# A hybrid attention block on one core: 184 TensorE transposes replaced by VectorE block transposes with a transfer between partitions, and the two ends of SBUF exchanged

## The chip, the cores and the metric

The kernel runs on one core of one Trainium2 chip. The metric is the device time of one execution in microseconds (us), lower is better.

## The reference, cut to what matters

One layer of a hybrid block on 256 tokens of 2048 channels, all in float32. Three mixers read the same projection: sparse attention (NSA), a state-space mixer (SSD) and retention. Their results are merged by gates, added to the residual, and a gated feed-forward layer (FFN) with 5632 hidden channels follows.

```
u = rms_norm(x, norm_mix)
proj = u @ w_in                                   # 2048 x 16952
y_nsa, y_ssd, y_ret = nsa(..), ssd(..), retention(..)
g_nsa, g_ssd, g_ret = split(sigmoid(merge_g), 3)
merged = g_nsa*(y_nsa @ p_nsa) + g_ssd*(y_ssd @ p_ssd) + g_ret*(y_ret @ p_ret)
x = x + merged @ w_out
f = rms_norm(x, norm_ffn)
x = x + (silu(f @ w_gate) * (f @ w_up)) @ w_down
return rms_norm(x, norm_final)
```

## The kernel before

**Streams.** Every large product is a call of `stream` (L182 to L227): 256 tokens times a strip of up to 512 columns of one weight matrix. The weights come from HBM in tiles `raw` of 256 rows by 512 columns (0.5 MB, SP's queue, four buffers). ScalarE (ACT) rounds a tile to a short format, `wh` (L134, `act`), VectorE (DVE) subtracts for the rest, `wl` (L209); `wh` and `wl` have four buffers each. Activations stand in the same way as a pair, transposed so that channels lie on partitions: `uh`/`ul` (normed input), `ysh`/`ysl` (SSD), `ynh`/`ynl` (NSA), `yrh`/`yrl` (retention), `mh`/`ml` (merged), `fh`/`fl` (FFN input), `hh`/`hl` (FFN hidden). For each 128 channels and each half of the tokens TensorE (PE) does three matmuls at L221: high by high, high by low, low by high; the activations are the operand that stays in the array, 512 columns of `wh` or `wl` pass through. A tile of weights so feeds 12 matmuls. The names in a profile row are output<-weights,activations.

The order of the streams: the projections for SSD (with the four SSD groups in between), for NSA, then `merge` of SSD (with NSA's attention in between), the projections for retention, `merge` of NSA and of retention, `w_out`, eleven pairs of `w_gate` and `w_up`, and `w_down` in four strips of 44 times 128 channels.

**Side tasks.** Work beside the streams is written as generators in the queues `urgent`, `steady` and `slow`; after each third matmul `pump` takes one step. A step is one small matmul or transpose; `pause(n)` lets n steps pass. A scheduler then orders each engine's instructions by its own clock; each engine runs its list in order.

**Transposes.** A result comes out with tokens on partitions and has to be turned before it is an operand of the next stream. `to_features` (L238, SSD result `y`, retention result `yy`, residual `x2`) and `task_halves` (L894, `merged` and FFN hidden `hb`) do it for 512 channels by eight PE transposes of 128x128 in float32 (L163, tiles `tf` and `hv`) into PSUM; ACT then writes the high part and DVE the low part. There are 4 such turns for SSD, 2 for retention, 4 for `merged`, 4 for `x2` and 11 for `hb`.

**Places in SBUF.** Pools are stacks that grow from the left end (low addresses) or, with `side="right"`, from the right end (the top, 224 KB in a partition). In the built program before, the weights `raw`, `wh`, `wl` lie at 20 to 68 KB, `uh`/`ul` and `fh`/`fl` at 68 to 100, `ynh`/`ynl` at 116 to 132; on the right lie `ysh`/`ysl` at 192 to 224, `yrh`/`yrl` at 208 to 224, `mh`/`ml` at 176 to 208, `hh` at 136 to 180 and `hl` at 180 to 224. In NSA's attention the operands lie at 136 to 181 (keys and queries) and 144 to 160 KB (values and probabilities).

Of the kernel before, what the change touches and what calls it, by code (L numbers as in the profile page):

```python
# [10 lines left out]
F32 = mybir.dt.float32  # L11
# [89 lines left out]
def _build(tc, a):  # L101
# [13 lines left out]
        p = es.enter_context(tc.tile_pool(name=name, bufs=bufs, **kw))  # L115
        return p, es

    cp, _c = pool("const")
    ctx.enter_context(_c)
    rawp, _c = pool("raw", 4)  # L120
    ctx.enter_context(_c)
    hlp, _c = pool("hl", 4)
    ctx.enter_context(_c)
# [9 lines left out]
    def act(out, in_, func, **kw):  # L133
        nc.scalar.activation(out, in_, func, **kw)  # L134
# [53 lines left out]
    def pause(n):  # L188
        for _ in range(n):
            yield  # L190
# [58 lines left out]
                V.scalar_tensor_tensor(dl[:, k, :], pv, sv, dh[:, k, :], OP.mult, OP.subtract)  # L249


    uh = ap_.tile([P, KD, S], F32R, tag="ah", name="uh")
    ul = ap_.tile([P, KD, S], F32R, tag="al", name="ul")
    xt_pool, xt_es = pool("xt")
    xT = xt_pool.tile([P, KD, S], F32, name="xT")
    xsq = xt_pool.tile([P, 2, S], F32, name="xsq")
    xTr = a["xT"].rearrange("(k p) t -> p k t", p=P)
# [37 lines left out]
        stream(uh, ul, KD, w_in, c0, n, evac, **kw)  # L295


    bp, b_es = pool("bigT", side="right")
    ysh = bp.tile([P, KD, S], F32R, tag="bh", name="ysh")
    ysl = bp.tile([P, KD, S], F32R, tag="bl", name="ysl")  # L300
    np1, np1_es = pool("nsa1", side="right")

    def evac_to(get, scale=None):
        box = []
# [69 lines left out]
        square_x(k)  # L374
    row_norm(hps[1][0][:, 256:258])
    xt_es.close()
    sp_, s_es = pool("ssd")
# [151 lines left out]
    def task_z(g, zg):  # L529
        y = ys[g]  # L530
        sq = sp_.tile([P, 4], F32, tag="sq", name="sq")
        for t in range(NT):
            th = sp_.tile([P, 512], F32, tag="th", name="thz", bufs=2)
            act(th, zg[:, t, :], AF.Tanh)
            V.scalar_tensor_tensor(zg[:, t, :], th, 1.0, zg[:, t, :], OP.add, OP.mult)
            V.tensor_tensor(y[:, t, :], y[:, t, :], zg[:, t, :], OP.mult)
            act(zg[:, t, :], y[:, t, :], AF.Square, accum_out=sq[:, t:t + 1])
        rsqrt(sq[:, 2:4], sq[:, 0:2], 1.0 / 512, EPS)
        for t in range(NT):
            V.tensor_scalar(y[:, t, :], y[:, t, :], sq[:, 2 + t:3 + t], None, OP.mult)  # L540
        yield from pause(14)
        yield from to_features(y, 0, R("ssdn"), 4 * g, ysh, ysl, 4 * g)

    for g in range(4):
        steady.append(task_decay(g))
# [22 lines left out]
    kTl = np2.tile([P, 2, 2, S], F32R, name="kTl")
# [329 lines left out]
    def task_halves(src, c0, dh, dl, k0, scale):  # L898
        yield from pause(6)
        for t in range(NT):  # L900
            ps = aux("hv")
            for b in range(4):
                transpose(ps[:, b * P:(b + 1) * P], src[:, t, c0 + b * P:c0 + (b + 1) * P])
                yield
            pv = ps.rearrange("p (b q) -> p b q", b=4)
            o = (slice(None), slice(k0, k0 + 4), slice(t * P, (t + 1) * P))
            act(dh[o], pv, AF.Copy, scale=scale)
            if scale == 1.0:
                V.tensor_tensor(dl[o], pv, dh[o], OP.subtract)
            else:  # L910
                V.scalar_tensor_tensor(dl[o], pv, scale, dh[o], OP.mult, OP.subtract)
# [10 lines left out]

    def open_x2():
        g_es.close()
        ny_es.close()
        m_es.close()
        x2p, box["x2es"] = pool("x2")
# [3 lines left out]
        box["tmp"], box["tmpes"] = pool("ftmp")  # L931

    def task_f(c):
        yield from pause(4)
        yield from to_features(box["x2"], c * 512, R("nffn"), c * 4, fh, fl, c * 4)

    for c in range(4):
        cs = slice(c * 512, (c + 1) * 512)

        def ev_o(t, ps):  # L940
            if c == 0 and t == 0:
                open_x2()
            x2 = box["x2"]
            V.tensor_tensor(x2[:, t, cs], x2[:, t, cs], ps, OP.add)
# [15 lines left out]
    hl = hp_.tile([P, KF, S], F32R, name="hl")  # L960
    for i in range(11):
        hbox = []

        def ev_g(t, ps):
            if not hbox:
                hbox.append(tmp_p.tile([P, NT, 512], F32, tag="hb", name="hb", bufs=2))
            th = tmp_p.tile([P, 512], F32, tag="jk", name="fth", bufs=2)
            act(th, ps, AF.Tanh, scale=r2[:, 1, t:t + 1])
            V.scalar_tensor_tensor(hbox[0][:, t, :], th, 1.0, ps, OP.add, OP.mult)
        stream(fh, fl, KD, a["w_gate"], i * 512, 512, ev_g)  # L970
        hb = hbox[0]

        def ev_u(t, ps):
# [72 lines left out]
```

## Time and profile before

| | |
|---|---|
| time, median of 3 runs | 1860.78 us (1860.46 to 1861.12) |
| the profiled execution | 1862.26 us, of which 1860.5 us are the span of its instructions |
| PE busy | 1848.1 us, 99% of the span |
| DVE, ACT, POOL busy | 1044.0 us (56%), 855.0 us (46%), 59.8 us (3%) |
| HBM read | 342.35 MB, 185 GB/s over the span |

The span runs from the first to the last instruction of one execution. An engine is busy while an instruction of it runs; matmuls overlap, so that the start of one to the start of the next says what one costs, and its length does not.

### The profile page before, as it was taken

Reading aid. Unit: us, or ns where it says so; the run is one execution under the profiler, and the core shown is the slowest. Engines: PE = TensorE matmul, PEld = TensorE weight load, DVE = VectorE, ACT = ScalarE, POOL = GpSimd, SP = SyncE. Lnnn points to the kernel's source line nnn. Section 1 sums busy time; section 2 is a strip of 40 time slices with the busy share of each in tenths; the row PEclk is TensorE's granted clock in tenths of the full one; section 3 lists DMA queues with packets and bytes.
Section 4 is the critical chain, followed back from the end, with each engine's and each line's share of the span. In section 5 each row is a group of like instructions: output and inputs, shape, how many; then the busy total and the mean of one; then the engine's idle time right before and its main releaser. Section 6 shows DMA issues by size and latency. Waiting matters only on the chain.

```text
span 1860.5 us, 22303 instructions
## 1 busy us (share of the span) xinstructions
PE 1848.1 (99%) x8584; PEld 1521.1 (82%) x8584; DVE 1044.0 (56%) x1209; ACT 855.0 (46%) x1092; POOL 59.8 (3%) x75
## 2 busy tenths in 40 slices
PE   9999999999999999999999999999999999999998
PEld 8878888987877888888888888888888888888886
DVE  7688875456555445544555555555555555544443
ACT  7555554454544444544444444444444444443442
POOL 0000001000000001010100100000000000000000
PEclk9999999999999999999999999999999999999999
DMA  9466655754545665666666656666666666655554
GB/s 343 116 210 185 182 160 151 230 170 148 155 149 176 188 179 168 184 194 193 193 186 185 227 181 191 191 186 190 192 183 191 189 186 191 212 186 190 191 188 132
DMA packets 176539, 345.95 MB, mean 186 GB/s; under 512 B 10880, under 2 KB 17152, under 8 KB 175792
## 3 DMA queue, kind: packets, MB, share of 16 engines
q1 hardware_dynamic: 173312, 331.60, 59.0%
q0 software_dynamic: 2688, 12.23, 1.9%
q8 instruction: 67, 1.10, 0.2%
q10 hardware_dynamic: 432, 0.70, 0.1%
q14 instruction: 40, 0.33, 0.1%
HBM read 342.35 MB, written 2.13 MB: 185 GB/s over the span
## 4 chain that ended last, share of the span: by engine, by line
PE 98%; DVE 1%; issue 0%; ACT 0%; POOLq 0%; POOL 0%; DVEq 0%
PE mp L221 90%; PE hp L370 3%; PE yd L518 1%; PE hv L163 1%; PE c L619 1%; PE tf L163 0%; PE pT L163 0%; PE cv L163 0%; PE ny L585 0%; DVE erow L477 0%; PE ny L587 0%; PE ny L589 0%; PE hp L345 0%; PE yo L523 0%; DVE wl L209 0%
## 5 line engine op out<-in xcount | busy, mean ns | idle before, releaser
L209 DVE TENSOR_TENSOR wl<-raw,wh 128x1024 fp32r<-128x1024 f32 (+2 forms) x616 | 748.4, 1216 | 717.5 <-ACT wh L134 717.0
L134 ACT ACTIVATE wh<-raw 128x1024 fp32r<-128x1024 f32 (+2 forms) x616 | 646.6, 1050 | 839.9 <-PE mp L221 776.1
L221 PE MATMUL mp<-wh,uh 128*128 128x512 f32 (+2 forms) x1024 | 408.1, 401 | 0.0
L221 PE MATMUL mp<-wl,uh 128*128 128x512 f32 (+2 forms) x1024 | 396.3, 387 | 2.1 <-DVE wl L209 2.1
L221 PE MATMUL mp<-wh,ul 128*128 128x512 f32 (+2 forms) x1024 | 396.2, 387 | 0.0
L221 PE MATMUL mp<-wh,fh 128*128 128x512 f32 x704 | 281.6, 400 | 0.0
L221 PE MATMUL mp<-wh,fl 128*128 128x512 f32 x704 | 274.5, 390 | 0.0
L221 PE MATMUL mp<-wl,fh 128*128 128x512 f32 x704 | 274.3, 390 | 0.0
L221 PEld LDWEIGHTS mp<-wh,uh 128*128 128x128 f32 x1024 | 193.3, 189 | 40.3 <-issue 1.6
L221 PEld LDWEIGHTS mp<-wh,ul 128*128 128x128 f32 x1024 | 193.1, 189 | 38.2 <-issue 0.7
L221 PEld LDWEIGHTS mp<-wl,uh 128*128 128x128 f32 x1024 | 193.5, 189 | 36.4 <-DVE wl L209 2.5
L221 PEld LDWEIGHTS mp<-wh,fh 128*128 128x128 f32 x704 | 132.2, 188 | 32.0
L221 PEld LDWEIGHTS mp<-wh,fl 128*128 128x128 f32 x704 | 132.2, 188 | 27.9
L221 PEld LDWEIGHTS mp<-wl,fh 128*128 128x128 f32 x704 | 132.5, 188 | 24.2
L221 PE MATMUL mp<-wh,hh 128*128 128x512 f32 x352 | 139.5, 396 | 0.0
L221 PE MATMUL mp<-wh,hl 128*128 128x512 f32 x352 | 138.9, 395 | 0.0
L221 PE MATMUL mp<-wl,hh 128*128 128x512 f32 x352 | 138.9, 395 | 0.0
L221 PEld LDWEIGHTS mp<-wh,hh 128*128 128x128 f32 x352 | 66.3, 188 | 15.8
L221 PEld LDWEIGHTS mp<-wh,hl 128*128 128x128 f32 x352 | 66.3, 188 | 15.6
L221 PEld LDWEIGHTS mp<-wl,hh 128*128 128x128 f32 x352 | 66.3, 188 | 15.1
L221 PE MATMUL mp<-wh,mh 128*128 128x512 f32 x128 | 52.5, 410 | 0.0
L221 PE MATMUL mp<-wh,ysh 128*128 128x512 f32 x128 | 51.1, 399 | 0.0
(300 smaller groups left out, 1655.9 us busy)
## 6 DMA issues: line engine op xcount, KB each, us to landing
raw<-in_w_in_dram SPq DMA_DIRECT2D x240, 512.0 KB, 3.6
raw<-in_w_gate_dram SPq DMA_DIRECT2D x88, 512.0 KB, 3.7
raw<-in_w_up_dram SPq DMA_DIRECT2D x88, 512.0 KB, 3.7
raw<-in_w_down_dram SPq DMA_DIRECT2D x88, 512.0 KB, 4.7
raw<-in_p_ssd_dram SPq DMA_DIRECT2D x32, 512.0 KB, 3.7
raw<-in_w_out_dram SPq DMA_DIRECT2D x32, 512.0 KB, 4.3
raw<-in_p_nsa_dram SPq DMA_DIRECT2D x16, 512.0 KB, 3.8
raw<-in_p_ret_dram SPq DMA_DIRECT2D x16, 512.0 KB, 3.7
```

Source lines behind the costliest of these rows:

```text
L134: nc.scalar.activation(out, in_, func, **kw)
L163: nc.tensor.transpose(out, in_, ident[:n, :n])
L209: V.tensor_tensor(wl[:, ks, :n], raw[:, ks, :n], wh[:, ks, :n], OP.subtract)
L221: mm = nc.tensor.matmul(o, xx[:, k, ts], ww[:, kk, :n], start=(k == 0 and i == 0), stop=(k == K - 1 and i == 2))
L370: nc.tensor.matmul(hps[c][t][:, 0:n], xx[:, k, ts], ww[:, c0:c0 + n], start=(k == 0 and i == 0), stop=(k == KD - 1 and i == 2))
L518: nc.tensor.matmul(ps[:, h * 64:(h + 1) * 64], erow[:, h, t, :], xdt[:, t, h * 64:(h + 1) * 64], start=True, stop=True)
L619: nc.tensor.matmul(ps[:, 0:NC2], wq[:, l, :], blk[b][:, 8 * q + l, :], start=(q == 0 and l == 0), stop=(q == 3 and l == 7))
```

## The change

Two things change.

1. **Sides.** The pools `const`, `raw`, `xt`, `ssd`, `merge`, `mgate`, `nsa2`, `x2` and `ftmp` go to the right end, and `bigT`, `nsa1`, `rety`, `ret`, `mT` and `hT` to the left. NSA's result (`nsay`) is opened before `bigT`, so it lies lowest of these. In the built program `wh`/`wl` now lie at 16 to 48 KB, `uh`/`ul` and `fh`/`fl` at 48 to 80, `ynh`/`ynl` at 80 to 96, `ysh`/`ysl` at 96 to 128, `yrh`/`yrl` at 96 to 112, `mh` at 112 to 128, `ml` at 128 to 144, `hh` at 80 to 124, `hl` at 124 to 168, `raw` at 204 to 220 KB.
2. **Turns.** Of the 25 turns 23 are done by a new `task_exchange`: all of SSD, retention and `hb`, and the first three quarters of `merged` and `x2`. DVE transposes 32x32 blocks of 512 channels into `tq` (two instructions, one for each half of the tokens), 16 transfers on POOL's queue of 32 rows of 1 KB each move the blocks to their partitions (`st_x`), and after `pause(24)` DVE applies the scale where there is one, ACT writes the high part and DVE the low part, now from SBUF and for 1024 elements at once. The last quarters of `merged` and `x2` keep PE's transposes. The factor 0.5 of `merged` moves to the addition after `w_out`, an instruction that is there anyway.

```
-    cp, _c = pool("const")
+    cp, _c = pool("const", side="right")
-    rawp, _c = pool("raw", 4)
+    rawp, _c = pool("raw", 4, side="right")
...
+    def exchange(pl, src, queue, tag="tq", bufs=1):
+        tq = pl.tile([P, 4, 8, 32], F32, tag=tag, name="tq", bufs=bufs)
+        st = pl.tile([P, 4, 8, 32], F32, tag="xs", name="st_x", bufs=1)
+        for t in range(NT):
+            V.transpose(tq.rearrange("p b (f t) q -> p t f b q", t=NT)[:, t], src[:, t, :].rearrange("p (f b q) -> p f b q", f=4, b=4))
+        for x in range(4):
+            for b in range(4):
+                queue.dma_start(st[32 * b:32 * b + 32, x], tq[32 * x:32 * x + 32, b])
+        return st
...
+    def task_exchange(pl, src, dh, dl, k0, scale=None, gap=24, **kw):
+        st = exchange(pl, src, nc.gpsimd, **kw)
+        yield from pause(gap)
+        oh, ol = quarters(dh, k0, 4), quarters(dl, k0, 4)
+        if scale is not None:
+            for f in range(4):
+                v = st.rearrange("p a (f t) q -> p f a (t q)", f=4)[:, f]
+                V.tensor_scalar(v, v, scale[:, f:f + 1], None, OP.mult)
+        act(oh, st, AF.Copy)
+        V.tensor_tensor(ol, st, oh, OP.subtract)
...
-    bp, b_es = pool("bigT", side="right")
+    nyp, ny_es = pool("nsay")
+    bp, b_es = pool("bigT")
...
-        yield from pause(14)
-        yield from to_features(y, 0, R("ssdn"), 4 * g, ysh, ysl, 4 * g)
+        yield from task_exchange(sp_, y, ysh, ysl, 4 * g, R("ssdn")[:, 4 * g:4 * g + 4])
...
-        yield from pause(8)
-        yield from to_features(yy, c * 512, R("retn"), 4 * c, yrh, yrl, 4 * c)
+        yield from task_exchange(rp, yy[:, :, cs], yrh, yrl, 4 * c, R("retn")[:, 4 * c:4 * c + 4])
...
-    mtp, mt_es = pool("mT", side="right")
+    mtp, mt_es = pool("mT")
...
+        if c < 3:
+            yield from pause(2)
+            yield from task_exchange(mtp, merged[:, :, c * 512:(c + 1) * 512], mh, ml, c * 4)
+            return
...
-    hp_, h_es = pool("hT", side="right")
+    hp_, h_es = pool("hT")
...
-        urgent.append(task_halves(hb, 0, hh, hl, 4 * i, 1.0))
+        urgent.append(task_hidden(hb, i))
```

On PE, in the second `w_gate` strip of the FFN, before (operands: `cst` holds the identity, `hb` the hidden channels of the strip ahead; eight rows of `hv` stand in the strip, two are shown):

```order
L221 MATMUL mp_9132<-wh,fh 128x512
L221 MATMUL mp_9132<-wl,fh 128x512
L221 MATMUL mp_9132<-wh,fl 128x512
L163 MATMUL hv<-cst,hb 128x128
L221 MATMUL mp_9131<-wh,fh 128x512
L221 MATMUL mp_9131<-wl,fh 128x512
L221 MATMUL mp_9131<-wh,fl 128x512
L163 MATMUL hv<-cst,hb 128x128
```

In the change no row of `hv` with `hb` is left on PE; of its rows in all, 8133 become 8001 as the listing counts them (runs of the same row counted once).

On DVE, at the same place, before (L974 is the end of a `w_up` strip, L909 writes the low part of the turned strip, L969 is the end of the next `w_gate` strip):

```order
L974 SCALAR_TENSOR_TENSOR hb<-hb,r_8109,mp_8984 128x512
L209 TENSOR_TENSOR wl<-raw,wh 128x1024 x3
L909 TENSOR_TENSOR hl<-hv,hh 128x4x128
L209 TENSOR_TENSOR wl<-raw,wh 128x1024
L909 TENSOR_TENSOR hl<-hv,hh 128x4x128
L209 TENSOR_TENSOR wl<-raw,wh 128x1024 x4
L969 SCALAR_TENSOR_TENSOR hb<-fth,mp_9131 128x512
```

and now (L1010, L1005 and L277 are the lines that answer to L974, L969 and L909):

```order
L1010 SCALAR_TENSOR_TENSOR hb<-hb,r_8181,mp_9080 128x512
L257 STREAM_TRANSPOSE tq<-hb 128x4x4x32
L209 TENSOR_TENSOR wl<-raw,wh 128x1024
L257 STREAM_TRANSPOSE tq<-hb 128x4x4x32
L209 TENSOR_TENSOR wl<-raw,wh 128x1024 x7
L1005 SCALAR_TENSOR_TENSOR hb<-fth,mp_9227 128x512
L209 TENSOR_TENSOR wl<-raw,wh 128x1024
L1005 SCALAR_TENSOR_TENSOR hb<-fth,mp_9228 128x512
L277 TENSOR_TENSOR hl<-st_x,hh 128x4x8x32
```

The two transposes stand right behind the end of `w_up`, and eight weight tiles lie between the second of them and the first use of what the transfers bring. ACT's reader (`hh<-st_x`) stands at the same place. Between transposes and first use lie 7 to 10 weight tiles in all 23 turns; the shortest, 7, is that of the first half of retention:

```order
L257 STREAM_TRANSPOSE tq<-yy 128x4x4x32 x2
L209 TENSOR_TENSOR wl<-raw,wh 128x1024 x7
L902 SCALAR_TENSOR_TENSOR rg<-rth,rg 128x512 x2
L903 TENSOR_TENSOR yy<-yy,rg 128x512
L275 TENSOR_SCALAR st_x<-st_x,prm 128x4x64 x4
```

On POOL the transfers stand between its other work, in the stretch from the merge of retention to the end (before, this list had no L260 rows; `merged` is the addition of a gated product, `x` the residual's load):

```order
L260 DMA st_x<-tq 32x256 x16
L815 TENSOR_TENSOR merged<-merged,gt 128x512 x2
L956 DMA x_8347<-in_x_dram 128x2x512 x4
L260 DMA st_x<-tq 32x256 x48
L167 TENSOR_SCALAR r_8181<-r_8181 128x2
L168 TENSOR_TENSOR r_8181<-r_8181,mhalf 128x2
L260 DMA st_x<-tq 32x256 x160
L1016 DMA nfb<-in_norm_final_dram 128x2048
L260 DMA st_x<-tq 32x256 x16
```

In that list every transfer from the ninth of a turn on waits for the one eight places before it to land, and the first of a turn waits for the readers of the turn before, since `st_x` has one buffer in each pool.

## Rows read from the trace of the kernel before

**Rows 1.** The page: busy time by engine; the chain that ended last, by engine.
```profile
PE 1848.1 (99%) x8584; PEld 1521.1 (82%) x8584; DVE 1044.0 (56%) x1209; ACT 855.0 (46%) x1092; POOL 59.8 (3%) x75
PE 98%; DVE 1%; issue 0%; ACT 0%; POOLq 0%; POOL 0%; DVEq 0%
```

**Rows 2.** Groups by line: PE's matmuls with `wl`, count, busy us, mean ns.
```profile
L221 PE MATMUL mp<-wl,fh 128*128 128x512 f32 x704 | 274.3, 390 | 0.0
L221 PE MATMUL mp<-wl,hh 128*128 128x512 f32 x352 | 138.9, 395 | 0.0
L221 PE MATMUL mp<-wl,ysh 128*128 128x512 f32 x128 | 50.5, 395 | 0.0
L221 PE MATMUL mp<-wl,mh 128*128 128x512 f32 x128 | 50.4, 394 | 0.0
L221 PE MATMUL mp<-wl,yrh 128*128 128x512 f32 x64 | 25.2, 394 | 0.0
L221 PE MATMUL mp<-wl,ynh 128*128 128x512 f32 x64 | 24.9, 389 | 0.0
L587 PE MATMUL ny<-pT,vth 128*128 128x512 f32 x12 | 4.7, 394 | 0.0
```

**Rows 3.** Stretches: busy us and count by engine, granted clock; NSA's merge, then `w_down`.
```profile
782.00:902.00 120.00, 120.00 (x531) 99.36 (x530) 60.04 (x52) 50.60 (x51) 14.11 (x8) 1.00 0.65 193
1640.00:1840.00 200.00, 200.00 (x863) 162.14 (x862) 95.68 (x88) 79.63 (x84) 0.00 (x0) 1.00 0.58 184
```

**Rows 4.** Timeline of PE: start, length; first transposes of some turns.
```profile
299.71 1.03 PE L163 MATMUL tf<-cst,y 128*128 128x128 f32 x8
300.58 0.60 PE L163 MATMUL kc<-cst,kc 128*128 128x128 f32 x4
...
1050.20 0.27 PE L163 MATMUL tf<-cst,x 128*128 128x128 f32 x1
...
1073.38 0.27 PE L163 MATMUL tf<-cst,x 128*128 128x128 f32 x1
...
1164.14 0.27 PE L163 MATMUL hv<-cst,hb 128*128 128x128 f32 x1
...
1208.70 0.27 PE L163 MATMUL hv<-cst,hb 128*128 128x128 f32 x1
```

**Rows 5.** Groups by line: DVE and ACT instructions like those added and removed.
```profile
L909 DVE TENSOR_TENSOR hl<-hv,hh 128x512 fp32r<-128x512 f32 x22 | 15.2, 692 | 0.9
L134 ACT ACTIVATE hh<-hv 128x512 fp32r<-128x512 f32 x22 | 13.2, 600 | 14.6 <-PE hv L163 14.6
L540 DVE TENSOR_SCALAR y<-y,sq 128x512 f32<-128x512 f32 x8 | 3.5, 483 | 1.7 <-POOL sq L168 1.7
```

**Rows 6.** Timelines of ACT and DVE in a `w_gate` strip; brackets: idle before, releaser.
```profile
1148.69 1.06 ACT L134 ACTIVATE wh<-raw 128x1024 fp32r<-128x1024 f32 x1 [1.66 <-PE mp L221]
1149.79 1.23 DVE L209 TENSOR_TENSOR wl<-raw,wh 128x1024 fp32r<-128x1024 f32 x1 [1.50 <-ACT wh L134]
```

**Rows 7.** Timeline of POOL: start, length; issues of transfers, and two arithmetic instructions.
```profile
88.39 0.71 POOL L441 DMA_DIRECT2D adram<-act_t  x1 [30.49 <-DVE act_t L440]
303.39 0.56 POOL L613 DMA_DIRECT2D w<-in_cmp_v_w_dram  x1
330.31 0.88 POOL L617 DMA_DIRECT2D wq<-in_cmp_v_w_dram  x1 [3.75 <-DMA wq<-in_cmp_k_w_dram]
693.56 0.58 POOL L168 TENSOR_TENSOR bn<-bn,mhalf 128x1 f32<-128x1 f32 x1
695.64 1.43 POOL L168 TENSOR_TENSOR bn<-bn,mhalf 128x1 f32<-128x1 f32 x1
```

**Rows 8.** Transfers: KB each, median us from issue to landing.
```profile
wq<-in_cmp_v_w_dram POOLq DMA_DIRECT2D x4, 512.0 KB, 5.3
adram<-act_t POOLq DMA_DIRECT2D x1, 32.0 KB, 2.5
```

More of the change, by code (lines that the diff above doesn't have):

```diff
@@ L249, in to_features, with quarters @@
                 V.scalar_tensor_tensor(dl[:, k, :], pv, sv, dh[:, k, :], OP.mult, OP.subtract)
+    def exchange(pl, src, queue, tag="tq", bufs=1):
[7 more added lines that the diff above has]
+        return st
+    def quarters(d, k, n):
+        return d[:, k:k + n, :].rearrange("p f (t a q) -> p a (f t) q", t=NT, a=4)
+    def task_exchange(pl, src, dh, dl, k0, scale=None, gap=24, **kw):
[8 more added lines that the diff above has]
+        V.tensor_tensor(ol, st, oh, OP.subtract)
     uh = ap_.tile([P, KD, S], F32R, tag="ah", name="uh")
     ul = ap_.tile([P, KD, S], F32R, tag="al", name="ul")
-    xt_pool, xt_es = pool("xt")
+    xt_pool, xt_es = pool("xt", side="right")
     xT = xt_pool.tile([P, KD, S], F32, name="xT")
@@ L295, in proj @@
         stream(uh, ul, KD, w_in, c0, n, evac, **kw)
-    bp, b_es = pool("bigT", side="right")
+    nyp, ny_es = pool("nsay")
+    bp, b_es = pool("bigT")
     ysh = bp.tile([P, KD, S], F32R, tag="bh", name="ysh")
     ysl = bp.tile([P, KD, S], F32R, tag="bl", name="ysl")
-    np1, np1_es = pool("nsa1", side="right")
+    np1, np1_es = pool("nsa1")
     def evac_to(get, scale=None):
@@ L376, in _build @@
     xt_es.close()
-    sp_, s_es = pool("ssd")
+    sp_, s_es = pool("ssd", side="right")
     bt = sp_.tile([P, NT, 512], F32, tag="t4a", name="bt")
@@ L558, in _build @@
     s_es.close()
-    mpool, m_es = pool("merge")
+    mpool, m_es = pool("merge", side="right")
     merged = mpool.tile([P, NT, D], F32, name="merged")
-    nyp, ny_es = pool("nsay")
     ynh = nyp.tile([P, 8, S], F32R, name="ynh")
     ynl = nyp.tile([P, 8, S], F32R, name="ynl")
-    gp, g_es = pool("mgate")
-    np2, np2_es = pool("nsa2")
+    gp, g_es = pool("mgate", side="right")
+    np2, np2_es = pool("nsa2", side="right")
     kTh = np2.tile([P, 2, 2, S], F32R, name="kTh")
@@ L802, in _build @@
     b_es.close()
-    ryp, ry_es = pool("rety", side="right")
+    ryp, ry_es = pool("rety")
     yrh = ryp.tile([P, 8, S], F32R, name="yrh")
     yrl = ryp.tile([P, 8, S], F32R, name="yrl")
-    rp, r_es = pool("ret", side="right")
+    rp, r_es = pool("ret")
     cstr = rp.tile([P, _CSTR.shape[1]], F32, name="cstr")
@@ L893, in _build, with task_merged @@
     r_es.close()
-    mtp, mt_es = pool("mT", side="right")
+    mtp, mt_es = pool("mT")
     mh = mtp.tile([P, KD, S], F32R, name="mh")
     ml = mtp.tile([P, KD, S], F32R, name="ml")
-    def task_halves(src, c0, dh, dl, k0, scale):
+    def task_merged(c):
+        if c < 3:
+            yield from pause(2)
+            yield from task_exchange(mtp, merged[:, :, c * 512:(c + 1) * 512], mh, ml, c * 4)
+            return
         yield from pause(6)
@@ L902, in task_halves @@
             for b in range(4):
-                transpose(ps[:, b * P:(b + 1) * P], src[:, t, c0 + b * P:c0 + (b + 1) * P])
+                transpose(ps[:, b * P:(b + 1) * P], merged[:, t, (4 * c + b) * P:(4 * c + b + 1) * P])
                 yield
             pv = ps.rearrange("p (b q) -> p b q", b=4)
[L906 to L911, printed above, removed]
+            o = (slice(None), slice(4 * c, 4 * c + 4), slice(t * P, (t + 1) * P))
+            act(mh[o], pv, AF.Copy)
+            V.tensor_tensor(ml[o], pv, mh[o], OP.subtract)
     merge(2, yrh, yrl, 8, a["p_ret"],
-          after=lambda c: urgent.append(task_halves(merged, c * 512, mh, ml, c * 4, 0.5)))
+          after=lambda c: urgent.append(task_merged(c)))
     fh = ap_.tile([P, KD, S], F32R, tag="ah", name="fh")
@@ L924, in open_x2 @@
         g_es.close()
-        ny_es.close()
         m_es.close()
-        x2p, box["x2es"] = pool("x2")
+        x2p, box["x2es"] = pool("x2", side="right")
         box["x2"] = x2p.tile([P, NT, D], F32, name="x2")
@@ L930, in open_x2 @@
             nc.gpsimd.dma_start(box["x2"][:, :, c * 512:(c + 1) * 512], xres[:, :, c * 512:(c + 1) * 512])
-        box["tmp"], box["tmpes"] = pool("ftmp")
+        box["tmp"], box["tmpes"] = pool("ftmp", side="right")
     def task_f(c):
-        yield from pause(4)
-        yield from to_features(box["x2"], c * 512, R("nffn"), c * 4, fh, fl, c * 4)
+        if c < 3:
+            yield from pause(2)
+            yield from task_exchange(box["tmp"], box["x2"][:, :, c * 512:(c + 1) * 512], fh, fl, c * 4,
+                                     R("nffn")[:, 4 * c:4 * c + 4], tag="hb", bufs=2)
+        else:
+            yield from pause(4)
+            yield from to_features(box["x2"], c * 512, R("nffn"), c * 4, fh, fl, c * 4)
     for c in range(4):
@@ L943, in ev_o @@
             x2 = box["x2"]
-            V.tensor_tensor(x2[:, t, cs], x2[:, t, cs], ps, OP.add)
+            V.scalar_tensor_tensor(x2[:, t, cs], ps, 0.5, x2[:, t, cs], OP.mult, OP.add)
             jk = box["tmp"].tile([P, 512], F32, tag="jk", name="jk", bufs=2)
@@ L957, in _build, with task_hidden @@
     ry_es.close()
-    hp_, h_es = pool("hT", side="right")
+    ny_es.close()
+    hp_, h_es = pool("hT")
     hh = hp_.tile([P, KF, S], F32R, name="hh")
     hl = hp_.tile([P, KF, S], F32R, name="hl")
+    def task_hidden(hb, i):
+        yield from pause(2)
+        yield from task_exchange(tmp_p, hb, hh, hl, 4 * i, tag="hb", bufs=2)
     for i in range(11):
```

## The prediction

> **What bounds the kernel now.** I read the page first. PE is busy for 99% of the span, and the chain of work that ended last runs 98% through PE [rows 1]. No stage waits for weights, DVE or ACT, so the time is the sum of what PE's instructions cost one after the other. A microsecond comes off only if PE gets fewer instructions or cheaper ones, and added work elsewhere costs only where PE comes to wait for it.
>
> What a matmul costs is read from starts, not lengths. A stretch of the stretches view counts matmuls that reach into it, so its width plus one length (0.39 us) over the count is the pitch: in NSA's merge (120.00 + 0.39) / 531 = 0.2267 us, in `w_down` (200.00 + 0.39) / 863 = 0.2322 us [rows 3]. Both have a granted clock of 1.00, so the 5.5 ns between them are not the clock. The groups by line show the same split in the lengths: 389 to 390 ns with `fh` and `ynh` as activations, 394 to 395 ns with `ysh`, `yrh`, `mh`, `hh` [rows 2]. The split follows the tile: within one merge it changes with the stream. What the slow tiles have in common is their place. All of them lie on the right, at 136 KB or higher; the fast ones lie on the left and end at 132 KB. NSA's own products, with both operands at 144 to 160 KB, have 394 ns too [rows 2]. What differs otherwise (length of the stream, who wrote the tile, the work of DVE and ACT beside it) is the same for some fast and slow tile.
>
> **The change part by part.**
>
> *Removed transposes.* 23 of 25 turns leave PE, eight transposes each, 184. Their cost on the path is again read from starts. In SSD eight stand back to back: from 299.71 to the next instruction at 300.58, 0.87 us [rows 4]. In the FFN a turn begins every 44.56 us (1164.14 to 1208.70 [rows 4]) with 192 matmuls between; 192 x 0.2267 = 43.53, so a turn costs 1.03 us. Among the slow matmuls of `w_out` it is 1050.20 to 1073.38, 23.18 us [rows 4], less 96 x 0.2322 = 22.29, so 0.89 us. I give SSD's 4 turns 0.87 each (3.5), the 4 that stand in slow streams (3 of `x2`, the last of `hb`) 0.89 (3.6), and the other 15 (retention, `merged`, `hb`) 1.03 (15.5). Sum: 22.5 us. Were all at the lowest price it would be 20.0, at the highest 23.7.
>
> *Places.* `ysh`/`ysl` feed 4 x 96 matmuls, `yrh`/`yrl` 4 x 48, `mh`/`ml` 4 x 96, `hh`/`hl` 4 x 264: 2016. Were they all to fall to the fast pitch, 2016 x 5.5 ns = 11.1 us. Somewhere between 132 and 136 KB the price changes; I take 134. In the changed program `ysh`, `ysl`, `yrh`, `yrl`, `mh` and `hh` lie below it. Of `ml` (128 to 144 KB) 10 of 16 channel blocks lie above, of `hl` (124 to 168) 34 of 44: 80 + 272 = 352 matmuls stay slow if the price belongs to the single matmul. 1664 x 5.5 ns = 9.2 us. No row shows fast and slow mixed; if one slow operand spoils its whole group of three, another 2 x 352 x 5.5 ns = 3.9 us stay and the term is 5.3. Ends: 0 and 11.1; I take 9.2.
>
> *DVE and ACT.* The block transpose stands in no row. Per 128x512 I bound it by 0.48 us (one input) and 1.23 us (a weight tile, twice the size), and take 0.69, the price of a 128x512 result of this shape [rows 5, 6]. An FFN turn then costs DVE 2 x 0.69 + 1.23 in place of 2 x 0.69, so 1.2 us more in 44 us, in a stage where it has half its time free (60.04 of 120 busy [rows 3]). ACT writes 1024 elements in 1.06 us in place of 2 x 0.60 [rows 5, 6]. Cost 0, covered by the lead of these engines: ACT starts a weight tile the moment PE frees its buffer, DVE ends it at 1149.79 + 1.23 = 1151.02, and PE has three more tiles of 12 x 0.2267 = 2.72 us to go through, to 1148.69 + 8.16 = 1156.85 [rows 6]. The lead is 5.8 us; a stall of DVE or ACT longer than that reaches PE.
>
> *The transfers.* They are what could make such a stall: ACT and DVE run in order, and `wh` and `wl` of the following tiles are queued behind the instruction that waits for `st_x`. An issue on POOL of the same shape (32 rows of 1 KB) took 0.71 us and landed in 2.5; others took 0.56 and 0.88, the slowest landing is 5.3 [rows 7, 8]. A turn is 16 x 0.71 + 2.5 = 13.9 us after the transposes; bounds 16 x 0.56 + 2.5 = 11.5 and 16 x 0.88 + 5.3 = 19.4. Waiting for the transfer eight places earlier adds nothing as long as eight issues (4.5 us and more) outlast most of a landing. Seven tiles of weights lie between at the least, 19.0 us, in the FFN eight, 21.8 us. So even the upper bound overruns the shortest gap by 0.4 us, inside the lead. Cost 0. POOL's own work is pushed back by one turn (11 us) at most: the additions to `merged` come every 33 us, the residual's load stands ahead of its transfers, and the load for the last norm is needed only in `w_down`. If the lead were gone, a turn late by d would cost d each time.
>
> *The rest.* The factor 0.5 moves into an addition that is there anyway: 0. The scale costs DVE four short instructions where the transposes' eviction had it: in the lead.
>
> Sum: 22.5 + 9.2 = 31.7 us less. Against the profiled execution's own 1862.26 us (span 1860.5 and 1.8 around it) that is 1830.6. The median of the runs shown is 1.5 us below it (1860.78), so I forecast **1829 us** for the median.
>
> **Rivals.**
>
> 1. *The place does nothing*: the 5.5 ns come from something else that goes with these tiles, and only the transposes count. 1860.8 - 22.5 = 1838. For it: no row shows one tile at two places. Against it: nine kinds of operand fall on the right side of one boundary. The Trainium skill, "SBUF — State Buffer", section "Who interferes with whom", speaks for this rival: TensorE has its own read ports and waits for nobody, and it names no cost of an address. By that page the sum would be 22.5 us alone. The trace has two pitches at one clock that the page does not explain, so I believe the rows.
>
> 2. *Mixed streams stay slow* (the group of three): 1860.8 - 22.5 - 5.3 = 1833.
>
> 3. *The transfers come late, and the kernel is slower.* One mechanism: POOL's issues are held up beside DVE. For it: the same small instruction on POOL took 0.58 and 1.43 us [rows 7], so something there can hold POOL for 0.85 us. Were each issue 0.71 + 0.85 = 1.56 us, an FFN turn would take 16 x 1.56 + 2.5 = 27.5 us against 21.8 + 5.8 = 27.6 that are covered: just nothing. From there each 0.1 us more per issue costs 1.6 us a turn and 37 us over 23. At 1.65 us the gain is gone; at 1.8 us (16 x 1.8 + 2.5 - 27.6 = 3.7 us x 23 = 85) the time would be 1860.8 - 31.7 + 85 = 1914. Against it: the issues shown took 0.56 to 0.88 beside the same DVE work. The Trainium skill, the same page, section "SBUF: two separate sides", warns of this trap: transfers issued from POOL need it to write descriptors, and DVE instructions in a two-port mode lock it out. No run shown here lengthens an issue that way.
>
> 4. *Part of the gain is lost to new stalls* in the SSD groups, where DVE is busiest and the scheduler has dealt out all side work anew, or to a late turn now and then: 1840 to 1857.
>
> **How the numbers follow.** A difference of 0.2% (3.7 us) is about what a measurement of this kernel can tell from none. Chances: the forecast (1826 to 1832) 0.55; rival 1 0.2; rival 2 0.12; rival 4 0.07; rival 3 0.06. The range of 8 in 10 must take in the forecast, rival 2 and most of rival 1, with the ends of the transposes' price: at the bottom all tiles fast and the highest price, 1860.8 - 23.7 - 11.1 = 1826; at the top rival 1 with the lowest price, 1860.8 - 20.0 = 1841. I give 1825 to 1841. The first three cases are faster by over 0.2%, and rival 4 nearly so; with a little left for it at the bound, faster 0.93, within 0.2% 0.02, slower 0.05.
>
> **What would show it.** PE with 184 fewer matmuls and still 99% busy; turns that begin 43.5 us apart in the FFN. `mp<-wl,ysh`, `yrh`, `mh` and `hh` at 389 ns instead of 394, `w_down` at a pitch of 0.2267 to 0.229; lengths of 394 there are rival 1, and a pitch of 0.230 or more with `hl` mixed in rival 2. Issues of `st_x` at 0.6 to 0.9 us, and ACT and DVE with no wait for `st_x` above a few us in all; waits of 6 us or more at each turn, followed by PE waiting for `wl`, are rival 3. Wrong would be a PE that waits for `wh` or `wl` in the SSD groups, or transposes of DVE far above 1.2 us.

## Result and the profile after

The change takes 1827.21 us (median of 4 runs, 1825.79 to 1828.67) against 1860.70 us before (median of 4 runs, 1860.46 to 1861.12): ratio 0.982, 95% interval 0.9803 to 0.9837, 33.5 us less. The forecast was 1829 us, with a range of 1825 to 1841. The profiled execution took 1825.79 us with a span of 1823.7, where that of before took 1862.26 with 1860.5: as it happens the one lies 1.4 us under its median and the other 1.6 us over, so between the two traces there are 36.5 us.

The page of the change, busy time by engine and then the chain that ended last, answers to [rows 1]:

```profile
PE 1811.7 (99%) x8400; PEld 1502.6 (82%) x8400; DVE 1069.6 (59%) x1250; ACT 847.2 (46%) x1051; POOL 243.4 (13%) x443
PE 96%; issue 2%; DVE 1%; DMA 0%; POOL 0%; ACT 0%; POOLq 0%; DVEq 0%
```

PE has 184 instructions fewer and 36.4 us less to do. Outside its busy time the span has 12.0 us, before it had 12.4. The "issue 2%" that the chain now names is so no new idle time, only another way in which the chain was put down. So all that was won is work that PE no longer has, and nothing of it was given back as a wait.

The matmuls with `wl` in the groups by line, as in [rows 2]:

```profile
L221 PE MATMUL mp<-wl,fh 128*128 128x512 f32 x704 | 274.0, 389 | 0.0
L221 PE MATMUL mp<-wl,hh 128*128 128x512 f32 x352 | 137.0, 389 | 0.0
L221 PE MATMUL mp<-wl,ysh 128*128 128x512 f32 x128 | 49.9, 390 | 0.0
L221 PE MATMUL mp<-wl,mh 128*128 128x512 f32 x128 | 49.8, 389 | 0.0
...
L221 PE MATMUL mp<-wl,ynh 128*128 128x512 f32 x64 | 24.9, 389 | 0.0
L221 PE MATMUL mp<-wl,yrh 128*128 128x512 f32 x64 | 24.9, 389 | 0.0
```

All are at 389 to 390 ns; the split of [rows 2] is gone. The stretches of NSA's merge and of `w_down`, as in [rows 3], say the same in starts:

```profile
767.00:877.00 110.00, 110.00 (x487) 91.11 (x486) 57.78 (x53) 48.24 (x49) 12.15 (x8) 1.00 0.66 197
1580.00:1780.00 200.00, 200.00 (x884) 165.64 (x883) 98.45 (x91) 82.77 (x87) 7.05 (x15) 1.00 0.64 199
```

(110.00 + 0.39) / 487 = 0.2267 us and (200.00 + 0.39) / 884 = 0.2267 us. `w_down`, which had 0.2322, holds 884 matmuls in the 200 us where it held 863. The low parts stand in the groups with `wh`; `hl` and `ml`, the two tiles that reach highest, are as fast as the others:

```profile
L221 PE MATMUL mp<-wh,hl 128*128 128x512 f32 x352 | 137.0, 389 | 0.0
...
L221 PE MATMUL mp<-wh,ml 128*128 128x512 f32 x128 | 49.9, 389 | 0.0
```

The turns in the FFN, on POOL's timeline (start, length, count, and in brackets the idle time before and what ended it):

```profile
1144.00 5.48 POOL L260 DMA_DIRECT2D st_x<-tq  x11 [44.70 <-ACT wh L134]
1149.80 2.45 POOL L260 DMA_DIRECT2D st_x<-tq  x5 [0.32 <-DMA st_x<-tq]
1187.50 5.45 POOL L260 DMA_DIRECT2D st_x<-tq  x11 [35.26 <-ACT wh L134]
```

A turn begins every 1187.50 - 1144.00 = 43.50 us, where [rows 4] had 44.56: the 192 matmuls between two turns cost 43.53 and nothing else is left on PE. The prices of the new work, which no row of before held, stand in the groups by line: the issues on POOL, and DVE's block transpose of half a strip of `hb` (one half of the tokens).

```profile
L260 POOL DMA_DIRECT2D st_x<-tq x368 | 182.0, 502 | 479.4 <-ACT wh L134 360.9 <-DVE tq L257 39.9 <-DVE fl L277 29.4
...
L257 DVE STREAM_TRANSPOSE tq<-hb 128x512 f32<-128x512 f32 x22 | 15.4, 702 | 0.0
```

The list of issues (KB each, median us to landing) has the transfer itself:

```profile
st_x<-tq POOLq DMA_DIRECT2D x368, 32.0 KB, 4.0
```

The transpose took 0.70 us (0.69 was taken), an issue 0.50 (0.71 was taken from [rows 7]), a landing 4.0 (2.5 was taken from [rows 8]). One turn: 16 x 0.50 + 4.0 = 12.0 us behind the transposes, where 13.9 was worked out. In the list of waits (us in total, times, longest) PE has two in all, and the one for the transfers is POOL's own, for the transfer eight places earlier:

```profile
POOL st_x L260 <- DMA st_x<-tq: 19.7, 40, 1.1
...
PE mp L221 <- DVE wl L209: 1.7, 1, 1.7
...
PE hp L374 <- DVE idle L289: 1.3, 1, 1.3
```

### The profile page after: what moved, and what is told of

Its sections match the earlier page's. It is cut to its first block, busy times and chain, and to the rows that moved or that the text cites. A ratio compares the mean times of both kernels' runs of the same rounds, so it can differ in the third digit from the quotient of the medians.

```text
span 1823.7 us, 22560 instructions
## 1 busy us (share of the span) xinstructions
PE 1811.7 (99%) x8400; PEld 1502.6 (82%) x8400; DVE 1069.6 (59%) x1250; ACT 847.2 (46%) x1051; POOL 243.4 (13%) x443
## 3 DMA queue, kind: packets, MB, share of 16 engines
q0 software_dynamic: 14464, 24.31, 4.0%
## 4 chain that ended last, share of the span: by engine, by line
PE 96%; issue 2%; DVE 1%; DMA 0%; POOL 0%; ACT 0%; POOLq 0%; DVEq 0%
PE mp L221 88%; PE hp L399 3%; PE yd L547 1%; PE c L646 1%; DMA erow<-adram 0%; PE pT L163 0%; PE ny L612 0%; DVE erow L506 0%; PE ny L614 0%; PE ny L616 0%; PE hp L374 0%; PE yo L552 0%; DVE wl L209 0%; PE xk L163 0%; PE st L540 0%
## 5 line engine op out<-in xcount | busy, mean ns | idle before, releaser
L221 PE MATMUL mp<-wh,uh 128*128 128x512 f32 (+2 forms) x1024 | 402.9, 398 | 0.0
L221 PE MATMUL mp<-wh,fh 128*128 128x512 f32 x704 | 274.5, 390 | 0.0
L260 POOL DMA_DIRECT2D st_x<-tq x368 | 182.0, 502 | 479.4 <-ACT wh L134 360.9
L815 POOL TENSOR_TENSOR merged<-merged,gt 128x512 f32<-128x512 f32 x16 | 29.2, 1845 | 181.8 <-DVE gt L814 181.8
```

Source lines behind the costliest of these rows:

```text
L221: mm = nc.tensor.matmul(o, xx[:, k, ts], ww[:, kk, :n], start=(k == 0 and i == 0), stop=(k == K - 1 and i == 2))
L260: queue.dma_start(st[32 * b:32 * b + 32, x], tq[32 * x:32 * x + 32, b])
L815: nc.gpsimd.tensor_tensor(merged[:, t, cs], merged[:, t, cs], gt[:, t, :], OP.add)
```

## Experiments

Each kernel was timed beside the kernel before on the same chip, and the differences below are taken to that. It had 1858.84 us there for the first four kernels, 1858.82 for the next four, 1860.40 for the three with powers and 1859.24 for the last.

**Which half of the change brings what, and what the pitch hangs on.** Two theories stood for the 5.5 ns: the *place* (height in the memory, as predicted), and a *remainder* (what is left of a tile's start address, counted within a partition, when it is divided by 256 bytes). In the program before, the weights `wh` and `wl` and the fast tiles begin at addresses with remainder 0x60 (96 bytes), the slow tiles on the right at 0xe0 (224). In the change all of them begin at 0x80 (128).

e1_pad_right: the kernel before, with one unused tile that moves everything on the right down by 640 bytes, so that the tiles stay at 135 KB and more but have remainder 0x60.

```diff
+    padp, _c = pool("pad", side="right")
+    ctx.enter_context(_c)
+    padp.tile([P, 160], F32, name="padr")
```

> The kernel before, with one unused tile of 640 bytes at the top of the right side, so that every tile on the right lies 640 bytes lower: ysh, yrh, mh, hh and their low parts stay at 135 KB and above, but their addresses now have the same remainder modulo 512 bytes as wh and wl have, as those of uh, fh and ynh always had. Theory 'place' (addresses above some height are slow; in the changed kernel hl at 124 to 168 KB is fast, so the height would have to be above 168 KB or the pairing decide): w_down stays at a pitch of 0.232 us, lengths of 394 to 395 ns, time 1860 to 1861 us. Theory 'remainder' (a matmul is slowed when the moving operand and the activations differ modulo 512): w_down at 0.2267 us, lengths 389 ns for ysh, yrh, mh, hh, time 1861 - 11 = 1850 us.

e2_sides_only: the pools on the sides that the change gives them, all transposes on PE as before.

```diff
-    cp, _c = pool("const")
+    cp, _c = pool("const", side="right")
...
-    bp, b_es = pool("bigT", side="right")
+    nyp, ny_es = pool("nsay")
+    bp, b_es = pool("bigT")
```

> The kernel before with the sides exchanged as in the change and every turn still on TensorE. My prediction's term of the places: 9.2 us less (bounds 0 and 11.1), 1851.5 us; by the trace of the changed kernel, in which all 2016 matmuls run at 0.2267 us but those of ysh beside the attention, 11 us less, 1850 us. The rival that the place does nothing: 1861 us, lengths of 394 ns.

e3_turns_only: the turns by DVE and transfers, the pools on their old sides (the lines of e2_sides_only the other way round).

> The change with the sides left as before: 23 turns by VectorE and transfers, tiles on the old sides. My prediction's term of the turns: 22.5 us less (bounds 20.0 and 23.7), 1838 us, w_down at 0.232 us. If the two parts help each other (transfers late, or matmuls disturbed by turns), the sum of this run's gain and of the sides' alone is not that of the whole change, 33.5 us.

e4_offsets: the whole change, with small unused tiles that give the activations different distances to the weights.

```diff
+    nyp.tile([P, 8], F32, name="pd0")
...
+    bp.tile([P, 8], F32, name="pd1")
...
+    ryp.tile([P, 56], F32, name="pd2")
...
+    mtp.tile([P, 32], F32, name="pd3")
...
+    hp_.tile([P, 32], F32, name="pd4")
```

> The changed kernel with small unused tiles on the left, so that the activations' addresses differ from those of wh and wl modulo 512 bytes: NSA's result by 32, SSD's by 64, hh and hl by 128, retention's by 256, merged by 384; all of them stay in the lower half. Theory 'place': nothing changes, all at 389 ns, time as the changed kernel, 1826 to 1829 us. Theory 'remainder': hh at least (128, the difference in the kernel before) at 394 to 395 ns and a pitch of 0.232 us, so 1056 x 5.5 ns = 5.8 us more, and up to 12 us more if all five are slowed; the lengths say which differences are slow.

Measured: e1_pad_right 1848.17 us (ratio 0.9939, 0.9927 to 0.9952), 10.7 us less than before. e2_sides_only 1848.40 (0.9941, 0.9928 to 0.9953), 10.4 less. e3_turns_only 1836.61 (0.9878, 0.9864 to 0.9891), 22.2 less. e4_offsets 1837.87 (0.9883, 0.9868 to 0.9898), 21.0 less, so some 12 us of the change's gain of 33.5 were gone. The two halves add up: 10.4 + 22.2 = 32.6 of 33.5 us.

One unused tile of 640 bytes in the old kernel does as much as mirroring the sides. In its groups by line the tiles, still on the right and still at 135 KB and more, are fast:

```profile
L224 PE MATMUL mp<-wl,hh 128*128 128x512 f32 x352 | 136.9, 389 | 0.0
L224 PE MATMUL mp<-wl,ysh 128*128 128x512 f32 x128 | 50.0, 391 | 0.0
```

In e3_turns_only the group of `hh` and the stretch of `w_down` are as before, though the transposes are gone from PE. So it was not the transposes' company that made them slow:

```profile
L221 PE MATMUL mp<-wl,hh 128*128 128x512 f32 x352 | 138.9, 395 | 0.0
...
1615.00:1815.00 200.00, 200.00 (x863) 162.14 (x862) 95.64 (x88) 79.34 (x84) 0.00 (x0) 1.00 0.56 184
```

In e4_offsets each distance has its price. All tiles lie within 0.5 KB of where the change has them. Against the weights `fh` lies at a multiple of 256 bytes, `ynh` 32 bytes beyond one, `ysh` 64, `hh` and `mh` 128, `yrh` a full 256:

```profile
L221 PE MATMUL mp<-wl,fh 128*128 128x512 f32 x704 | 273.9, 389 | 0.0
L221 PE MATMUL mp<-wl,hh 128*128 128x512 f32 x352 | 138.9, 395 | 0.0
L221 PE MATMUL mp<-wl,ysh 128*128 128x512 f32 x128 | 50.6, 395 | 0.0
L221 PE MATMUL mp<-wl,mh 128*128 128x512 f32 x128 | 50.5, 394 | 0.0
...
L221 PE MATMUL mp<-wl,ynh 128*128 128x512 f32 x64 | 25.3, 395 | 0.0
L221 PE MATMUL mp<-wl,yrh 128*128 128x512 f32 x64 | 24.9, 389 | 0.0
```

`yrh` is the only one that was moved and stayed fast, and the only one moved by 256. 32 bytes cost as much as 128, by the lengths. `w_down` is back at the old pitch: the stretch from 1610 to 1810 us holds 863 matmuls, (200.00 + 0.39) / 863 = 0.2322 us. The slow ones are 192 matmuls with `yn`, 384 with `ys`, 384 with `m` and 1056 with `h`: 2016 x 5.5 ns = 11.1 us.

**Distance or own remainder.** So far every fast tile of activations had a remainder of 0x60 or 0x80, and every slow one another. e5_shift128 moves weights and activations together to remainder 0; e6_all_aligned also puts the two operands of the header's products (`hp`, the first products of the kernel, with weight tiles `hwh` and `hwl` of their own) and of NSA's a multiple of 256 bytes apart.

```diff
+    padp, _c = pool("pad")
+    ctx.enter_context(_c)
+    padp.tile([P, 32], F32, name="padl")
...
-    gates = np2.tile([P, NT, 24], F32, name="gates")
+    gates = np2.tile([P, NT, 32], F32, name="gates")
```

(The first three lines are both kernels', the last two e6_all_aligned's alone, with `hraw`, `hwh` and `hwl` at 1088 columns in place of `HN`.)

> The whole change, with one unused tile of 128 bytes lowest on the left side, so that every tile there moves up by 128 bytes: weights and activations both have remainder 0 to 256 instead of 128, and their difference is still a multiple of 256. Theory 'difference': all streams stay at 389 ns and 0.2267 us from start to start, time as the change's, 1825 to 1830 us. Rival 'own remainder' (in all kernels so far activations at remainders 0x60 and 0x80 were fast, those at 0x00, 0xa0, 0xc0 and 0xe0 slow): all 7200 matmuls of 512 columns go to 0.2322, 7200 x 5.5 ns = 40 us more, about 1867 us.

> As the kernel with the shift, and the gates tile widened to 32 columns and the header's tiles to 1088 columns (same work), so that the operands of the header's and of NSA's products have differences of a multiple of 256 bytes too. Theory 'difference': the 512-column header products go from 393 to 389 ns and 0.231 to 0.2267 us, NSA's ny and ss from 392 to 396 ns to 389; 288 header and some 60 NSA products x about 4 ns is 1 to 1.5 us less than the change, 1824 to 1829 us, hardly more than can be measured. Rival 'own remainder': header and NSA do not move together with the difference; header slow at remainder 0.

e5_shift128 took 1825.73 us (0.9823, 0.981 to 0.9837), the same as the change, and its streams are fast:

```profile
L224 PE MATMUL mp<-wl,fh 128*128 128x512 f32 x704 | 273.9, 389 | 0.0
L224 PE MATMUL mp<-wl,hh 128*128 128x512 f32 x352 | 136.9, 389 | 0.0
```

So it is the distance of the two operands, not where either of them lies, among the distances that these kernels have: multiples of 256 bytes, and 32, 64 and 128 beyond one. e6_all_aligned took 1826.47 us (0.9829, 0.9815 to 0.9842): no gain over the change that can be told. Its groups show why; the header's products and NSA's did not become 389 ns with their operands a multiple of 256 apart:

```profile
L402 PE MATMUL hp<-hwl,uh 128*128 128x512 f32 x32 | 12.7, 396 | 0.0
...
L617 PE MATMUL ny<-pT,vth 128*128 128x512 f32 x12 | 4.7, 392 | 0.0
```

The expectation of 389 ns there was a miss. For the weight streams, 7200 matmuls, the distance is shown to decide; for the header and NSA something else sets the last few ns, and what it is stays open.

**Are the transfers covered?** The prediction costed them at nothing, with a cover of 21.8 us of weight tiles in the FFN and 5.8 us of lead. First two kernels in which they should not matter. e9_small_pieces lays `st_x` out so that each transfer writes runs of 128 bytes; e11_no_transfers leaves the exchange out (blocks stay where they are, so it computes something else).

```diff
-                queue.dma_start(st[32 * b:32 * b + 32, x], tq[32 * x:32 * x + 32, b])
+                queue.dma_start(st[32 * b:32 * b + 32, :, x], tq[32 * x:32 * x + 32, b])
...
-        return st
+        return tq
```

(The first pair is e9_small_pieces, the last e11_no_transfers, without the lines of the transfers.)

> The whole change, but the exchanged tile is laid out so that every transfer writes 256 pieces of 128 bytes instead of 32 of 1 KB; readers stand as before 8 weight tiles (22.3 us) behind the transposes, with a lead of 5.8 us. Cover theory: a turn (1.4 us of transposes, 16 issues, the last landing) costs nothing as long as it is under 28.1 us. If an issue stays below 0.9 us and a landing below 7 us, the time is the change's, 1825 to 1830 us. If an issue takes over 1.36 us with a landing of 5 us, each of the 20 odd turns is late by 16 times the excess, and TensorE waits for DVE's or ACT's halves: at 1.65 us some 4.6 us a turn, about 1930 us. Rival 'transfers disturb the streams': slower without any wait, by longer matmuls or later weight loads.

> The whole change without the exchange: the readers take the tile that DVE's block transposes wrote, so the 368 transfers (and the transposition between blocks) are left out and the numbers computed are others. Cover theory: the transfers cost nothing, the time stays 1825 to 1830 us. Rival 'part of the gain is lost to the transfers' (they hold POOL for 182 us and share the memory with weight loads): faster by 4 us or more, below 1823 us, with fewer idle times on TensorE.

e9_small_pieces took 1826.19 us (0.9827, 0.9814 to 0.984). Its issue cost 0.59 us, with landings of 3.9, and POOL's queue moved 14464 packets as in the change: the shorter runs did not become more packets, so this kernel tested little but 31 us more of POOL.

```profile
L260 POOL DMA_DIRECT2D st_x<-tq x368 | 212.9, 586 | 455.6 <-ACT wh L134 354.7 <-DVE tq L257 41.2 <-DVE fl L278 26.5
```

e11_no_transfers took 1825.61 us (0.9823, 0.981 to 0.9837): 368 transfers and 182 us of POOL gone, and nothing gained. Against e5_shift128, timed beside it with its transfers (1825.73), the difference is below what can be told. That settles rival 4 as far as the transfers go: no part of the gain is lost to them.

e12_delay8, e13_delay16 and e14_delay24 were to make a turn late by 6.8, 13.0 and 19.2 us, with powers on POOL ahead of the transfers (8, 16 and 24 of them).

```diff
+        dl = pl.tile([P, 2], F32, tag="dly", name="dly", bufs=1)
+        nc.gpsimd.tensor_scalar(dl[:, 0:1], tq[:, 3, 7, 31:32], 0.0, 1.0, OP.mult, OP.add)
+        for _ in range(24):
+            nc.gpsimd.tensor_tensor(dl[:, 1:2], dl[:, 0:1], mhalf[:, 0:1], OP.pow)
```

> The whole change, with 1 + 8 small powers of one column put on POOL between the block transposes and the transfers of each of the 23 turns (0.52 us and 8 x 0.78 us by the rows of the normalisation's powers on POOL, 6.8 us a turn); the readers stand at the same places in the order. In the profile of the change one FFN turn lands by about 1156.2 us and its first reader stands on ACT at 1163.5, so 7.3 us are spare before a reader waits, and TensorE has a lead of 5.8 us more. Cover theory: nothing waits, time as the change's, 1825 to 1830 us. Rival 'POOL is on the path': 23 x 6.8 = 156 us more.

> The same with 1 + 16 powers, 13.0 us a turn. Cover theory: the readers on ACT or DVE wait some 5.7 us in a full turn, TensorE's lead of 5.8 us just hides it; time between the change's and 1.5 us a turn more, 1826 to 1860 us, with waits of ACT or DVE for the transfers of st_x in the profile. Rival 'much more is spare': no such waits, 1825 to 1830 us.

> The same with 1 + 24 powers, 19.2 us a turn. Cover theory: each turn is late by 19.2 - 7.3 - 5.8 = 6.1 us for TensorE, in about 20 of the 23 turns, some 120 us, 1900 to 1970 us. Rival 'much more is spare, the order of the engines alone hides a turn': under 1840 us.

They took 1826.44 us (0.9817, 0.9804 to 0.983), 1826.25 (0.9821, 0.9808 to 0.9835) and 1828.58 (0.9829, 0.9815 to 0.9842). That refutes neither theory on the cover, since the delay didn't happen. POOL's timeline of e14_delay24 shows the transfers right behind the transposes, with one power among them and the rest after them, where the scheduler had put them:

```profile
1147.16 2.06 POOL L264 DMA_DIRECT2D st_x<-tq  x4 [0.60 <-ACT wh L134]
1149.24 0.57 POOL L261 TENSOR_TENSOR dly<-dly,mhalf 128x1 f32<-128x1 f32 x1
1149.77 4.94 POOL L264 DMA_DIRECT2D st_x<-tq  x10
```

What they do show: POOL can be busy for 700.4 us (the page of e14_delay24), nearly three times as long as in the change, and the transfers still arrive in time. The only new idle time on PE in e14_delay24 is 2.0 us for POOL's addition to `merged`.

e15_words makes the transfers themselves long. `st_x` is laid out so that the four source blocks alternate word by word, and the readers stand where they stood, eight weight tiles behind the transposes.

```diff
-        st = pl.tile([P, 4, 8, 32], F32, tag="xs", name="st_x", bufs=1)
+        st = pl.tile([P, 8, 32, 4, 1], F32, tag="xs", name="st_x", bufs=1)
...
-                queue.dma_start(st[32 * b:32 * b + 32, x], tq[32 * x:32 * x + 32, b])
+                queue.dma_start(st[32 * b:32 * b + 32, :, :, x], tq[32 * x:32 * x + 32, b].rearrange("p f (n w) -> p f n w", w=1))
```

> The powers of the three kernels before did not stand ahead of the transfers in the order, so they loaded POOL and delayed nothing. Here the transfers themselves are made longer: the whole change, but each transfer scatters single words (st_x laid out so that the four source blocks alternate word by word), and the readers, four pieces of 128x256 each on ACT and DVE, stand as before 8 weight tiles behind the transposes. How long such a transfer takes no row shows; the profile will. Cover theory: a turn may be 13.1 us longer than the change's (7.3 us spare before a reader waits, 5.8 us of lead) at no cost; beyond that each of some 20 turns costs TensorE the excess, with waits of ACT or DVE for the transfers of st_x in the list of waits: if issue and landing together take 25 us longer, 20 x 12 = 240 us more. Rival 'the order hides any turn': 1825 to 1835 us however long the transfers. Rival 'the engines of the transfers are shared': the weight loads land later and TensorE waits for raw instead.

It took 5274.62 us (ratio 2.8366, 2.8332 to 2.84). From its page, the busy times and the groups of the transfers and of the readers of `hb`'s turns:

```profile
PE 1876.5 (36%) x8400; PEld 1538.5 (29%) x8400; DVE 1095.3 (21%) x1319; ACT 868.5 (16%) x1120; POOL 1038.7 (20%) x443
...
L260 POOL DMA_DIRECT2D st_x<-tq x368 | 978.0, 2658 | 3179.3 <-issue 2785.1
...
L134 ACT ACTIVATE hh<-st_x 128x256 fp32r<-128x256 f32 x44 | 25.2, 644 | 1666.5 <-DMA st_x<-tq 1666.5
```

An issue takes 2.66 us and its transfer lands 9.9 us after it, by the list of issues; POOL's queue moved 55680 packets where it had 14464:

```profile
st_x<-tq POOLq DMA_DIRECT2D x368, 32.0 KB, 9.9
```

The 16 issues and one landing alone would be 16 x 2.66 + 9.9 = 52.5 us. A turn is longer because the issues stand some 10.6 us apart, each about when the transfer before it has landed; for the idle time of POOL between them the trace names no releaser ("issue"), so why they do not overlap stays open:

```profile
3006.81 2.66 POOL L260 DMA_DIRECT2D st_x<-tq  x1 [7.79 <-issue]
3017.36 2.65 POOL L260 DMA_DIRECT2D st_x<-tq  x1 [7.89 <-issue]
```

Here the cover is used up, and how large it is can be read from one turn of the FFN. The timelines of DVE, ACT and PE (the two block transposes; ACT's last piece of work before the reader and the reader; PE's first matmul after it):

```profile
2955.06 0.70 DVE L257 STREAM_TRANSPOSE tq<-hb 128x512 f32<-128x512 f32 x1
...
2956.79 0.70 DVE L257 STREAM_TRANSPOSE tq<-hb 128x512 f32<-128x512 f32 x1
...
2976.96 0.67 ACT L134 ACTIVATE fth<-mp,r 128x512 f32<-128x512 f32 x1
3129.15 2.29 ACT L134 ACTIVATE hh<-st_x 128x256 fp32r<-128x256 f32 x4 [151.52 <-DMA st_x<-tq]
...
3132.44 0.79 PE L221 MATMUL mp<-wh,fh 128*128 128x512 f32 x1 [145.61 <-ACT wh L134]
```

ACT comes to the reader at 2976.96 + 0.67 = 2977.63, 22.6 us after the turn began (in the change, 1141.01 to 1163.47, 22.5 us). The last transfer lands at 3129.15, 174.1 us after the turn began. PE runs on until 3132.44 - 145.61 = 2986.83, 9.2 us longer than ACT, and needs 3.3 us after the landing until the first weights are there: net 5.9 us. So of 174.1 us it stands still for 174.1 - 22.6 - 5.9 = 145.6. The prediction's cover was 21.8 us of tiles, counted from the end of the transposes, and a lead of 5.8. Counted so, ACT has 2977.63 - 2957.49 = 20.1 us, and with the 5.9 the cover is 26.0 us where 27.6 stood. No kernel made a turn just a little too long, so this border is worked out from one turn and was not crossed step by step.

Over the whole span PE's waits add up to 2041.2 (for `wh`) + 752.3 (for `wl`) + 297.4, 148.9 and 146.7 (for a few others) = 3386.5 us, all but some 10 us of it in 23 long waits, one a turn. PE's busy time is 64.8 us longer; together that is 3451.3 us, and the span is 3449.9 us longer than the change's. Waits for `raw` would speak for the rival of shared transfer engines. ACT has 72.2 us of them in all, none above 5.1 us, where it had 4.9 us in the change; whether sharing makes them or the bursts after each standstill is not shown, but PE's short waits leave that rival 10 us of 3450 at most. The 64.8 us are the clock, as far as this turn shows: on PE's timeline the first 12 matmuls after the wait take from 3132.44 to 3138.56, less 0.47 of waiting 5.65 us, in place of 12 x 0.2267 = 2.72, and 23 times the difference of 2.9 is 67. The stretches behind the wait of that turn (the number after the busy time and count is the granted clock):

```profile
3132.00:3137.00 5.00, 4.09 (x9) 0.50 0.44 116
3137.00:3147.00 10.00, 10.00 (x42) 0.92 0.77 258
```

After 145 us in which it had nothing to do, TensorE runs at 0.50, the lower level of 1.2 GHz, for the next 5 us and is back near the upper one in the 10 us after.

## Why the prediction was right, and where it wasn't

*What bounds the kernel.* Right. PE is at 99% before and after, and the time fell by what its instructions cost less.

*Removed transposes, 22.5 us.* Right: e3_turns_only measured 22.2, inside the bounds of 20.0 and 23.7. The price by starts (0.87 to 1.03 us a turn) rather than by the sum of eight lengths was the choice that made it: in the FFN a turn vanished from a period of 44.56 us and 43.50 were left.

*Places, 9.2 us.* The size was near, e2_sides_only measured 10.4, but by luck, for the reason was wrong. The step that failed is "somewhere between 132 and 136 KB the price changes; I take 134". There is no such height. `hl` ends at 168 KB and `ml` at 144, and by that step 352 matmuls of theirs would have stayed slow; `w_down` has 0.2267 us throughout. What decides is whether weights and activations lie a multiple of 256 bytes apart (e1_pad_right, e4_offsets, e5_shift128). The trace of before could not tell the two apart, since all tiles on the right also shared one remainder, but the addresses of the program had this second difference in them; the prediction weighed the heights in KB alone. With the right reason the term is all 2016 matmuls, 11.1 us; measured were 10.4 and 10.7. e4_offsets shows what was lucky: at the same heights, but with other remainders, the predicted step would still have given 9.2 us, and 2016 matmuls were slow.

The side of the memory matters only by the way: tiles of whole multiples of 256 bytes stacked from one end keep one remainder, tiles stacked from two ends have two, unless the ends happen to fit. Mirroring put weights and activations on the same side; 640 unused bytes did the same.

*DVE and ACT, 0.* Right, with 0.70 us for the block transpose where 0.69 was taken between 0.48 and 1.23.

*The transfers, 0.* Right. Issues were cheaper than the rows of before said (0.50 for 0.71) and landings slower (4.0 for 2.5), 12.0 us for 13.9. e11_no_transfers shows no cost of them that can be told, and one turn of e15_words that the cover which hides them is near the one that was worked out: 20.1 + 5.9 us behind the transposes, where 21.8 + 5.8 stood in the text.

*The rivals.* 1 (the place does nothing) falls by e2_sides_only, and yet it had something: it said that something else goes with these tiles. The Trainium skill, "SBUF — State Buffer", section "Who interferes with whom", by which TensorE waits for nobody, names no cost of an address; the two pitches at one granted clock stand beside it, and e1_pad_right shows that an address alone makes them. 2 (mixed streams stay slow) had no case, for no stream was mixed. 3 (issues held up on POOL) did not happen: the mean of 368 issues is 0.50 us beside a DVE that is busy for 59% of the span. The trap of which the Trainium skill, "SBUF — State Buffer", section "SBUF: two separate sides", warns is so not seen here; whether any instruction of DVE ran in the two-port mode that it names, no row shows. The condition of rival 3 was sound, though: what a turn takes beyond its cover goes to PE, as e15_words shows, where the span grew by 150 us for each of the 23 turns. 4 (gain given back as stalls) falls with PE's waits of 1.7 and 1.3 us.

## What to carry to other kernels

Where two groups of equal matmuls have different pitches at the same clock, compare the remainders of their operands' addresses as well as their places and their company: here a distance of a multiple of 256 bytes between weights and activations was worth 2.4% of each 512-column matmul, and a small unused tile bought it. Transposes on a bound TensorE can go to DVE blocks and transfers at no cost that could be measured here, as long as the readers stand far enough behind: count the tiles between, add the lead, and check that a turn (transposes, issues, last landing) is shorter. An experiment that is to delay something must be read in its trace first, since a scheduler may have moved the delay behind what it was to delay.

## What was not expected of the hardware

- The pitch of a stream of 512-column matmuls is 0.2267 us when the two operands lie a multiple of 256 bytes apart and 0.2322 us at 128 bytes beyond one; at 32 and 64 bytes beyond one the matmuls have the same length of 395 ns. No run here shows the mechanism, and the header's and NSA's products do not follow it.
- A transfer of 32 KB that scatters single words took 2.66 us to issue in place of 0.50 and 9.9 to land in place of 4.0, and a turn of 16 took 174 us in place of some 15, as the issues came one by one, some 10.6 us apart; with runs of 128 bytes it took 0.59 us and landed as before.
